# A decoder block in fp32r: SwiGLU in four parts instead of three, with the down products among the next part's blocks, seven of eleven hidden blocks in seven products, three lent PSUM banks and edges of order

## The chip, the cores and the metric

The kernel runs on one core of one Trainium2 chip. The metric is the device time of one execution in microseconds (us). Three executions of the kernel before took 1533.85, 1528.16 and 1534.53 us, median 1533.85. The engines are named as the profile names them: PE is TensorE, which multiplies; DVE is VectorE; ACT is ScalarE; POOL is GpSimd; SP is SyncE, which issues the weight loads.

## The reference

One decoder block on 256 tokens of width 2048, in float32. Cut to what matters:

```python
h = x + mixer(rmsnorm(x))          # w_in: 2048 x 16400, w_out: 2048 x 2048
h = h + swiglu(rmsnorm(h))         # w_gate_up: 2048 x 11264, w_down: 5632 x 2048
return rmsnorm(h)

def mixer(h):
    q, k, v, g_out, gk_low, gate_b, gate_c, xc, merge_a, merge_b = split(h @ w_in)
    # log decays from gk_low; chunked causal gated linear attention over 4 heads
    o = gla_chunked(q, k, v, log_sigmoid(gk_low @ w_gk_up + b_gk_up) / 16)
    y_a = rmsnorm(o) * silu(g_out)
    y_b = gate_b * causal_conv3(gate_c * xc)
    return (sigmoid(merge_a) * y_a + sigmoid(merge_b) * y_b) @ w_out

def swiglu(h):
    gate, up = split(h @ w_gate_up)          # 5632 columns each
    return (silu(gate) * up) @ w_down
```

## The kernel before, in words

**Three products for one.** A float32 product is made of three fp32r products. Each operand is split in a high part, rounded to fp32r, and a low part, the rest. `mm3` (L324 to L328) multiplies token-high by weight-low (L326), token-low by weight-high (L327) and high by high (L328) into one PSUM bank. In a row of the profile the weights stand first: `dn<-lo,acth` is L326.

**Pieces.** The weights are streamed in pieces of 128 partitions x 1024 floats (512 KB): two chunks of 128 rows by 512 columns. For each piece SP issues the load into `raw`, ACT makes the high part (L217) and DVE subtracts it to make the low part (L222). `take` (L314) keeps five pieces loaded ahead of the one in use (`LOOK = 5`); `raw` and `lo` have five buffers each, `hi` six. A plain piece costs PE 12 matmuls of 512 columns: two halves of the tokens (t = 0, 1), two chunks, three products.

**Eights and sevens.** A block is 512 columns of the gate and the same 512 of the up matrix, 16 plain pieces, 192 matmuls. The function `eights` (L354) does one matrix of it, in two PSUM banks, one for each half of the tokens. The function `sevens` (L374) does gate and up of one block together in seven products instead of eight (Strassen's scheme in Winograd's form, on token halves and row chunks): 28 pieces of 6 matmuls, 168 matmuls, in five banks `b0` to `b4`. For 16 of the 28 pieces the weights must first be added on DVE (`sum_of`, L238 and L244), and afterwards five results are combined on DVE (L398 to L411). `mixed` (L106) puts plain pieces between those of a seven: one behind each piece that needed a sum, the rest among the last eight.

**The order.** A list written out by hand (`stream_list`, L157) sets the order of all pieces: the attention's k, q and v columns; the gates (24 groups of 512 columns, four pairs of them in sevens); w_out; then SwiGLU. SwiGLU is done in three parts of 4, 4 and 3 blocks (`PARTS`, L69). In each part first the hidden blocks, some in sevens with others as eights between them (`HIDDEN`, L82: blocks 0, 2, 4, 6 and 9 in sevens), and then all down products of that part (`down_list`, L141), whose sums DVE adds to `h` (L1044). Small work is tied to the count of pieces used, the tick: `later` and `at` run a function at a tick, `one_at_a_time` runs the transposes of finished hidden blocks two ticks apart. A scheduler then arranges the instructions of each engine into its fixed order, and may move an instruction ahead of others that were written earlier.

**PSUM.** There are eight banks. `b0` to `b4` serve sevens. During gates and hidden blocks the eights always use `b5` and `ax1`, and the transposes `ax0` (L354 and L543). The down products take `b0` to `b5` in turn.

**Attention.** At ticks 20 to 25 tables of decays are made: POOL prepares `exk` and `exq` (L686 to L690), ACT takes the exponentials of four tables (L678, L691, L692, L705). `decayed` (L726) multiplies q and k by them, `scores` (L730) makes scores on PE and copies them out with a mask (L742 on DVE, L743 and L745 on ACT, L747 on DVE), and `attend` (L754) multiplies them by v into `o_ps`. `x_blocks` (L711, ticks 42, 47, 52, 57) makes the sums and differences of x that the gates' sevens need, on DVE (L715, L438, L440) and ACT (L439).

**The end.** The last 512 columns of the last part are two groups of 256. The second of them is done for t = 0 first and then for t = 1; `finish(t)` (L942) normalises and stores each half.

## Time and profile before

| what | value |
|---|---|
| median of three executions | 1533.85 us (1528.16 to 1534.53) |
| the profiled execution | 1535.26 us |
| its span, first to last instruction | 1533.6 us |
| PE busy | 1510.4 us, 98% of the span |
| DVE busy | 1173.5 us, 77% |
| ACT busy | 832.1 us, 54% |
| HBM read over the span | 338.45 MB, 222 GB/s with the writes |
| SwiGLU on PE, first to last matmul | 822 to 1526 us |

How to read it: busy time is the union of an engine's instructions. A matmul of 512 columns is recorded as 0.389 us long, but the next one starts before it ends, so the price of a matmul on PE is the time from start to start, which is had by dividing a stretch in which PE never waits by the matmuls in it. A view by waits names, for each engine and line, who released it and for how long it had been idle. A view by windows gives busy time, counts, the granted TensorE clock and the DMA traffic of stretches of the span.

### The profile page before, as it was taken

The page shows a single profiled execution, that of the slowest core. Times are in us where ns is not written, and L with a number is a line of the kernel's source. Part 1 is how long each engine was busy: PE and PEld are TensorE (multiplying, and loading weights), DVE is VectorE, ACT ScalarE, POOL GpSimd, SP SyncE. Part 2 cuts the span into 40 slices and gives each one's busy share as a digit, 9 for nine tenths or more (in the row PEclk, how much of TensorE's full clock was granted, in tenths as well). Part 3 has the DMA queues.
Part 4 walks back from the last instruction along what each step waited for, and adds up shares of the span by engine and source line. Part 5 has one row for each costly group of instructions (what it writes and reads, how often), then busy time and mean ns, then how long its engine had stood idle before and what let it go on. Part 6 is the DMA issues. An engine that isn't in the chain of part 4 may idle for free.

```text
span 1533.6 us, 19370 instructions
## 1 busy us (share of the span) xinstructions
PE 1510.4 (98%) x7153; PEld 1262.0 (82%) x7153; DVE 1173.5 (77%) x1173; ACT 832.1 (54%) x936; POOL 36.6 (2%) x61
## 2 busy tenths in 40 slices
PE   9989999999999999999999999999999999999998
PEld 8979988888787788878788888888888888888887
DVE  5787557979879879965668899855889975678764
ACT  6755445555654555654556555633555653455543
POOL 0020000000000000000000000000000000000000
PEclk9999999999999999999999999999999999999999
DMA  9645557878776888786765767866677886566872
GB/s 321 222 150 158 172 158 248 276 228 259 260 246 212 286 261 257 242 263 206 224 178 178 263 221 250 312 200 178 219 248 224 273 272 192 178 229 197 249 222 92
DMA packets 96399, 346.00 MB, mean 226 GB/s; under 512 B 11092, under 2 KB 11220, under 8 KB 96176
## 3 DMA queue, kind: packets, MB, share of 16 engines
q1 hardware_dynamic: 92928, 333.77, 68.0%
q0 software_dynamic: 2944, 9.41, 2.5%
q10 hardware_dynamic: 432, 1.57, 0.3%
q8 instruction: 56, 0.92, 0.2%
q14 instruction: 39, 0.32, 0.1%
HBM read 338.45 MB, written 2.10 MB: 222 GB/s over the span
## 4 chain that ended last, share of the span: by engine, by line
PE 92%; DVE 3%; issue 1%; ACT 1%; DMA 1%; POOL 1%; SPq 0%; DVEq 0%; ACTq 0%
PE fg L326 7%; PE fg L328 7%; PE fg L327 7%; PE dn L326 5%; PE dn L327 5%; PE dn L328 5%; PE gc L326 3%; PE fu L326 3%; PE fu L328 3%; PE fu L327 3%; PE gc L328 3%; PE gc L327 3%; PE gb L326 2%; PE wo L326 2%; PE mb L326 2%; PE gb L327 2%
## 5 line engine op out<-in xcount | busy, mean ns | idle before, releaser
L222 DVE TENSOR_TENSOR lo<-raw,hi 128x1024 fp32r<-128x1024 f32 (+1 forms) x517 | 628.1, 1219 | 231.3 <-PE dn L326 74.8
L217 ACT CAST hi<-raw 128x1024 fp32r<-128x1024 f32 (+1 forms) x517 | 539.9, 1050 | 409.1 <-PE dn L328 114.1
L217 ACT CAST hi<-x 128x1024 fp32r<-128x1024 f32 x108 | 113.7, 1053 | 185.6 <-DVE x L244 130.0
L222 DVE TENSOR_TENSOR lo<-x,hi 128x1024 fp32r<-128x1024 f32 x108 | 132.1, 1223 | 31.8 <-ACT hi L217 18.7
L326 PE MATMUL dn<-lo,acth 128*128 128x512 f32 (+1 forms) x376 | 141.7, 377 | 0.0
L328 PE MATMUL dn<-hi,acth 128*128 128x512 f32 (+1 forms) x376 | 141.3, 376 | 0.0
L327 PE MATMUL dn<-hi,actl 128*128 128x512 f32 (+1 forms) x376 | 141.2, 376 | 0.0
L326 PE MATMUL fg<-lo,hh 128*128 128x512 f32 x312 | 121.6, 390 | 0.0
L328 PE MATMUL fg<-hi,hh 128*128 128x512 f32 x312 | 121.5, 389 | 0.0
L327 PE MATMUL fg<-hi,hl 128*128 128x512 f32 x312 | 121.4, 389 | 0.0
L244 DVE TENSOR_TENSOR x<-x,raw 128x1024 f32<-128x1024 f32 x72 | 87.9, 1220 | 7.2 <-DMA raw<-in_w_in_dram 3.5
L328 PEld LDWEIGHTS dn<-hi,acth 128*128 128x128 f32 x376 | 70.8, 188 | 13.0
L326 PEld LDWEIGHTS dn<-lo,acth 128*128 128x128 f32 x376 | 70.8, 188 | 12.7
L327 PEld LDWEIGHTS dn<-hi,actl 128*128 128x128 f32 x376 | 70.8, 188 | 12.6
L328 PE MATMUL fu<-hi,hh 128*128 128x512 f32 x192 | 74.7, 389 | 0.0
L326 PE MATMUL fu<-lo,hh 128*128 128x512 f32 x192 | 74.7, 389 | 0.0
L327 PE MATMUL fu<-hi,hl 128*128 128x512 f32 x192 | 74.7, 389 | 0.0
L326 PEld LDWEIGHTS fg<-lo,hh 128*128 128x128 f32 x312 | 58.6, 188 | 12.5 <-DVE h L1044 0.3
L328 PEld LDWEIGHTS fg<-hi,hh 128*128 128x128 f32 x312 | 58.6, 188 | 12.4
L327 PEld LDWEIGHTS fg<-hi,hl 128*128 128x128 f32 x312 | 58.6, 188 | 12.1
L326 PE MATMUL fg<-lo,sh 128*128 128x512 f32 x160 | 63.8, 399 | 0.0
L328 PE MATMUL fg<-hi,sh 128*128 128x512 f32 x160 | 62.5, 391 | 0.0
(245 smaller groups left out, 3067.8 us busy)
## 6 DMA issues: line engine op xcount, KB each, us to landing
raw<-in_w_in_dram SPq DMA_DIRECT2D x255, 512.0 KB, 4.6
raw<-in_w_gu_dram SPq DMA_DIRECT2D x176, 512.0 KB, 4.4
raw<-in_w_dn_dram SPq DMA_DIRECT2D x88, 512.0 KB, 4.3
raw<-in_w_out_dram SPq DMA_DIRECT2D x32, 512.0 KB, 4.2
x<-in_w_gu_dram SPq DMA_DIRECT2D x20, 512.0 KB, 5.4
y<-in_w_gu_dram SPq DMA_DIRECT2D x20, 512.0 KB, 3.9
y<-in_w_in_dram SPq DMA_DIRECT2D x16, 512.0 KB, 4.2
x<-in_w_in_dram SPq DMA_DIRECT2D x16, 512.0 KB, 4.9
```

The costliest lines, as they stand in the source:

```text
L217: nc.scalar.copy(hi[:, ks, :], raw[:, ks, :])
L222: nc.vector.tensor_tensor(out=lo[:, ks, :], in0=raw[:, ks, :], in1=hi[:, ks, :].bitcast(F32), op=ALU.subtract)
L244: nc.vector.tensor_tensor(out=x, in0=x, in1=other, op=ALU.add)
L326: nc.tensor.matmul(ps, lhsT=sh, rhs=ml, start=first, stop=False, skip_group_check=onto)
L327: nc.tensor.matmul(ps, lhsT=sl, rhs=mh, start=False, stop=False, skip_group_check=onto)
L328: nc.tensor.matmul(ps, lhsT=sh, rhs=mh, start=False, stop=last, skip_group_check=onto)
```

## The change

Four things are changed.

**SwiGLU.** Parts of 3, 3, 3 and 2 blocks. Blocks 0, 3, 4, 6, 7, 9 and 10 are done in sevens. The others (1, 2, 5 and 8) and the down products of the first three parts form one list of plain pieces (`PLAIN`), of which each seven takes a number (`SEVENS`: 19, 19, 19, 19, 21, 17, 16). So a part's down products stand between the pieces of the next part's sevens. The last six down pieces of the third part follow the last seven; the fourth part's down products come at the end as before. A transpose of block f waits until the down products of block f - 4, whose buffer it takes, are through (`free_at`).

**Three lent banks.** `b5`, `ax0` and `ax1` form a queue. An eights group, and now a down group, takes the two at its front and gives them back at its end; a transpose takes the front one and puts it at the back. The rest of the program's turn goes over `b0` to `b4`.

**Edges of order.** `pin` keeps the written order of the first instruction of `x_blocks`, of the convolution's and of the merge's instructions on DVE, and `issue_after` puts the exponentials of `exk` and `exq` behind those of `ek` and `eq` on ACT.

**Ticks.** `x_blocks` runs at ticks 50, 54, 58 and 62.

```diff
-PARTS = ((0, 4), (4, 8), (8, 11))
+PARTS = ((0, 3), (3, 6), (6, 9), (9, 11))
...
-HIDDEN = (
-    ((("fg0", "fu0"), ("fg1", "fu1")), (("fg2", "fu2"), ("fg3", "fu3"))),
-    ((("fg4", "fu4"), ("fg5", "fu5")), (("fg6", "fu6"), ("fg7", "fu7"))),
-    ((("fg9", "fu9"), ("fg8", "fu8", "fg10", "fu10")),),
-)
+SEVENS = ((0, 19), (3, 19), (4, 19), (6, 19), (7, 21), (9, 17), (10, 16))
+PLAIN = (1, 2, (0, (1, 0, 2)), 5, (1, (3, 4, 5)), 8, (2, (6, 7, 8)))
...
+def hidden_list():
+
+    plain = []
+    for what in PLAIN:
+        if isinstance(what, tuple):
+            part, fs = what
+            plain += [e for n in range(len(DOWN[part])) for f in fs for e in down_of(part, n, f)]
+        else:
+            plain += [(f"{name}{what}", k) for name in ("fg", "fu") for k in range(0, KC, 2)]
+    out = []
+    for f, n in SEVENS:
+        out += mixed((f"fg{f}", f"fu{f}"), plain[:n])
+        plain = plain[n:]
+    return out + plain
...
-            tag = f"b{turn['b'] % 6}"
+            tag = f"b{turn['b'] % turn['of']}"
...
+    lent = ["b5", "ax0", "ax1"]
...
-    def eights(key, a, done, tags=("b5", "ax1")):
-
-        ps = [bank([P, 512], f"{key}_{t}", tag) for t, tag in enumerate(tags)]
+    def eights(key, a, done, tags=None):
+
+        mine = tags or [lent.pop(0) for _ in range(NT)]
+        ps = [bank([P, 512], f"{key}_{t}", tag) for t, tag in enumerate(mine)]
...
         done(ps)
+        if tags is None:
+            lent.extend(mine)
...
     def transpose_block(src, t, hi, lo):
 
-        ps = bank([P, 4, P], "trb", "ax0")
+        lent.append(lent.pop(0))
+        ps = bank([P, 4, P], "trb", lent[-1])
...
-        nc.scalar.activation(exk, exk, AF.Exp, scale=inv)
-        nc.scalar.activation(exq, exq, AF.Exp, scale=inv)
+        with tc.issue_after(first_exp[-1]):
+            nc.scalar.activation(exk, exk, AF.Exp, scale=inv)
+            nc.scalar.activation(exq, exq, AF.Exp, scale=inv)
...
-        nc.vector.tensor_tensor(out=raw, in0=xh[:, cs, :].bitcast(F32), in1=xl[:, cs, :].bitcast(F32), op=ALU.add)
+        pin(nc.vector.tensor_tensor(out=raw, in0=xh[:, cs, :].bitcast(F32), in1=xl[:, cs, :].bitcast(F32), op=ALU.add))
...
-        at(42 + 5 * q, lambda q=q: x_blocks(q))
+        at(X_AT[q], lambda q=q: x_blocks(q))
...
     def put(delay, f, src, t):
-        one_at_a_time(delay, lambda: transpose_block(src, t, *act_of(f)))
+        one_at_a_time(max(delay, free_at.get(f - 4, 0) - count["tick"]), lambda: transpose_block(src, t, *act_of(f)))
...
+    def down(key):
+
+        part, n = (int(s) for s in key[2:].split("_"))
+        cs = slice(DOWN[part][n][0], sum(DOWN[part][n]))
+        mine = [lent.pop(0) for _ in range(NT)]
+        ps = [bank([P, cs.stop - cs.start], f"{key}_{t}", tag) for t, tag in enumerate(mine)]
+        number = sum(e[0] == key for e in order)
+        for i in range(number):
+            piece, k0 = yield
+            for t in range(NT):
+                tok_piece(ps[t], t, piece, k0, i == 0, i == number - 1, hidden_act(part))
+        for t in range(NT):
+            nc.vector.tensor_tensor(out=h[:, t, cs], in0=ps[t], in1=h[:, t, cs], op=ALU.add)
+        lent.extend(mine)
...
+X_AT = (50, 54, 58, 62)
```

What this does to the order of the engines is seen at three places. A row is a line of the source, an operation, what it writes and reads, and a count where a row repeats; in the changed kernel the same line stands further down (L222 is L230, L244 is L252, L742 is L758).

The first place is ACT's queue at the decay tables. Before:

```order
L217 CAST hi<-raw 128x1024 x4
L691 ACT_TABLE_LOAD
L691 ACTIVATE exk<-exk 128x1024
L692 ACTIVATE exq<-exq 128x1024
L678 ACTIVATE ek<-eq 128x2048
L217 CAST hi<-raw 128x1024
L705 ACTIVATE eq<-eq 128x2048
L217 CAST hi<-raw 128x1024 x5
```

Now:

```order
L225 CAST hi<-raw 128x1024 x4
L693 ACT_TABLE_LOAD
L693 ACTIVATE ek<-eq 128x2048
L225 CAST hi<-raw 128x1024
L721 ACTIVATE eq<-eq 128x2048
L225 CAST hi<-raw 128x1024
L707 ACTIVATE exk<-exk 128x1024
L708 ACTIVATE exq<-exq 128x1024
L225 CAST hi<-raw 128x1024 x5
```

The two exponentials whose input POOL makes stood ahead of the two whose input DVE makes; they now stand behind them.

The second place is DVE's queue between the products of head 1 with the decay tables and the scores that are copied out of PSUM (`scr` is a score tile, `scl` its low part, `xraw` and `sl` belong to `x_blocks`). Before:

```order
L726 TENSOR_TENSOR exk<-exk,kr 128x256
L715 TENSOR_TENSOR xraw<-xh,xl 128x1024
L222 TENSOR_TENSOR lo<-raw,hi 128x1024
L438 TENSOR_TENSOR xraw<-xraw 128x256 x3
L222 TENSOR_TENSOR lo<-raw,hi 128x1024
L438 TENSOR_TENSOR xraw<-xraw 128x256
L222 TENSOR_TENSOR lo<-raw,hi 128x1024
L440 TENSOR_TENSOR sl<-xraw,sh 128x1024
L742 COPY_PREDICATED scr<-mask,sc_ps 128x256
L715 TENSOR_TENSOR xraw<-xh,xl 128x1024
L747 TENSOR_TENSOR scl<-scr,sch 128x384
```

Now:

```order
L742 TENSOR_TENSOR exk<-exk,kr 128x256
L230 TENSOR_TENSOR lo<-raw,hi 128x1024 x3
L758 COPY_PREDICATED scr<-mask,sc_ps 128x256
L763 TENSOR_TENSOR scl<-scr,sch 128x384
L230 TENSOR_TENSOR lo<-raw,hi 128x1024
L758 COPY_PREDICATED scr<-mask,sc_ps 128x256
L763 TENSOR_TENSOR scl<-scr,sch 128x384
```

The instructions of `x_blocks` have left this place for one some 20 pieces later.

The third place is DVE's queue where the second part's first down group ends (`h<-dn` is the addition of its sums to `h`, once for each half of the tokens). Before, in the stretch of down products alone:

```order
L222 TENSOR_TENSOR lo<-raw,hi 128x1024 x10
L1044 TENSOR_TENSOR h<-dn_0_0_10249,h 128x512
L222 TENSOR_TENSOR lo<-raw,hi 128x1024
L1044 TENSOR_TENSOR h<-dn_0_1_10250,h 128x512
L222 TENSOR_TENSOR lo<-raw,hi 128x1024
L1044 TENSOR_TENSOR h<-dn_1_0_10287,h 128x512
```

Now, among the pieces of block 7's seven:

```order
L252 TENSOR_TENSOR x<-x,raw 128x1024
L561 TENSOR_TENSOR actl<-trb,acth 128x4x128
L246 TENSOR_TENSOR raw<-y,x 128x1024
L230 TENSOR_TENSOR lo<-x,hi 128x1024
L230 TENSOR_TENSOR lo<-raw,hi 128x1024
L1021 TENSOR_TENSOR h<-dn_0_0_9676,h 128x512
L1021 TENSOR_TENSOR h<-dn_0_1_9677,h 128x512
L230 TENSOR_TENSOR lo<-y,hi 128x1024
L230 TENSOR_TENSOR lo<-raw,hi 128x1024
```

The additions now stand between the low parts and the sums of weights of a seven, and the banks that they free are two of the three lent ones, where before they were two of six.

More of the change, by code (lines that the diff above doesn't have):

```diff
@@ L103, in seven_list, with mixed @@
     return [(pair, e) for e in out + list(twos)]
-def mixed(step, early=False):
-    pair, keys = step
-    eights = [(key, k) for key in keys for k in range(0, KC, 2)]
+def mixed(pair, eights, early=False):
     if pair is None:
@@ L160, in stream_list @@
     out = [e for e in pieces if e[0][0] in "kqv"] + gates_list() + [e for e in pieces if e[0][:2] == "wo"]
-    for part in range(len(PARTS)):
-        out += hidden_list(part) + down_list(part)
-    return out
+    return out + hidden_list() + down_list()
 @with_exitstack
@@ L527, in transpose_gain @@
         for m in range(2):
-            ps = aux([P, 2, T], "tr")
+            lent.append(lent.pop(0))
+            ps = bank([P, 2, T], "tr", lent[-1])
             for j in range(2):
@@ L541, in transpose_block @@
     def transpose_block(src, t, hi, lo):
-        ps = bank([P, 4, P], "trb", "ax0")
+        lent.append(lent.pop(0))
+        ps = bank([P, 4, P], "trb", lent[-1])
         for j in range(4):
@@ L914, in block_kernel @@
     h = None
+    turn["of"] = 5
     for n in range(4):
@@ L967, in block_kernel @@
     act = {}
+    order = hidden_list()
+    base = count["tick"]
+    free_at = {f: base + 2 + max(i for i, e in enumerate(order) if e in down_of(p, len(DOWN[p]) - 1, f))
+               for p, fs in enumerate(PARTS[:-1]) for f in range(*fs)}
     def act_of(f):
@@ L1005, in hidden @@
         return eights(key, whole(hh, hl), gate_done)
-    finb = None
-    for part, (f0, f1) in enumerate(PARTS):
-        count["gap"] = 2
-        for _ in run(hidden_list(part), hidden):
-            pass
-        count["gap"] = 1
-        if part == len(PARTS) - 1:
-            finb = sT.tile([P, D], F32, tag="sh", name="finb")
-            nc.scalar.dma_start(finb, finw.to_broadcast([P, D]))
-        down = down_list(part)
-        of = {n: [e for e in down if e[0] == f"dn{part}_{n}"] for n in range(len(DOWN[part]))}
-        pd, kept = {}, {}
-        def hidden_act(t, k):
-            hi, lo = act_of(f0 + k // 4)
-            ts = slice(t * P, (t + 1) * P)
-            return hi[:, k % 4, ts], lo[:, k % 4, ts]
-        for e in down:
-            key, k0 = e
-            n = int(key.split("_")[1])
-            c0, w = DOWN[part][n]
-            cs = slice(c0, c0 + w)
-            last = part == len(PARTS) - 1 and n == nd - 1
-            if e == of[n][0]:
-                pd[n] = [bank([P, w], f"{key}_{t}") for t in range(NT)]
-            piece = take(key, k0)
-            if last:
-                kept[e] = piece
-                if e != of[n][-1]:
-                    continue
-            for t in range(NT):
-                for g in (of[n] if last else [e]):
-                    tok_piece(pd[n][t], t, kept[g] if last else piece, g[1], g == of[n][0], g == of[n][-1], hidden_act)
-                if e != of[n][-1]:
-                    continue
-                nc.vector.tensor_tensor(out=h[:, t, cs], in0=pd[n][t], in1=h[:, t, cs], op=ALU.add)
-                if part == len(PARTS) - 1:
-                    square_sum(h[:, t, cs], ssf[:, t, n:n + 1])
-                    if not last:
-                        nc.vector.tensor_tensor(out=h[:, t, cs], in0=h[:, t, cs], in1=finb[:, cs], op=ALU.mult)
-                    else:
-                        finish(t)
-            if not last:
-                used()
@@ new lines, in block_kernel @@
+    count["gap"] = 2
+    for _ in run(order, hidden):
+        pass
+    count["gap"] = 1
+    finb = sT.tile([P, D], F32, tag="sh", name="finb")
+    nc.scalar.dma_start(finb, finw.to_broadcast([P, D]))
+    part = len(PARTS) - 1
+    order = down_list()
+    of = {n: [e for e in order if e[0] == f"dn{part}_{n}"] for n in range(nd)}
+    acts = hidden_act(part)
+    pd, kept = {}, {}
+    for e in order:
+        key, k0 = e
+        n = int(key.split("_")[1])
+        c0, w = DOWN[part][n]
+        cs = slice(c0, c0 + w)
+        last = n == nd - 1
+        if e == of[n][0]:
+            pd[n] = [bank([P, w], f"{key}_{t}") for t in range(NT)]
+        piece = take(key, k0)
+        if last:
+            kept[e] = piece
+            if e != of[n][-1]:
+                continue
+        for t in range(NT):
+            for g in (of[n] if last else [e]):
+                tok_piece(pd[n][t], t, kept[g] if last else piece, g[1], g == of[n][0], g == of[n][-1], acts)
+            if e != of[n][-1]:
+                continue
+            nc.vector.tensor_tensor(out=h[:, t, cs], in0=pd[n][t], in1=h[:, t, cs], op=ALU.add)
+            square_sum(h[:, t, cs], ssf[:, t, n:n + 1])
+            if not last:
+                nc.vector.tensor_tensor(out=h[:, t, cs], in0=h[:, t, cs], in1=finb[:, cs], op=ALU.mult)
+            else:
+                finish(t)
+        if not last:
+            used()
```

48 lines of the change are left out of this document (27 added, 21 removed).

## The prediction

> **What bounds the kernel now.** I read the page first, then busy time by windows, then the waits of PE.
>
> ```profile
> PE 1510.4 (98%) x7153; PEld 1262.0 (82%) x7153; DVE 1173.5 (77%) x1173; ACT 832.1 (54%) x936; POOL 36.6 (2%) x61
> ```
>
> PE is busy 98% of 1533.6 us. Two windows split off SwiGLU; five of its stages follow (hidden blocks and down products of the first part, the same of the second, then the third's hidden blocks).
>
> ```profile
> 0.00:822.00 822.00, 806.42 (x3937) 676.95 (x3938) 630.18 (x652) 458.67 (x530) 36.65 (x61) 1.00 0.72 228
> 822.00:1526.00 704.00, 703.95 (x3218) 585.09 (x3216) 541.36 (x518) 371.94 (x402) 0.00 (x0) 1.00 0.70 222
> ...
> 822.00:989.50 167.50, 167.50 (x757) 138.46 (x756) 155.20 (x149) 104.84 (x117) 0.00 (x0) 1.00 0.77 252
> 989.50:1076.50 87.00, 87.00 (x387) 72.03 (x386) 49.04 (x46) 35.35 (x35) 0.00 (x0) 1.00 0.63 192
> 1076.50:1244.00 167.50, 167.50 (x753) 138.41 (x752) 153.02 (x143) 99.08 (x105) 0.00 (x0) 1.00 0.78 253
> 1244.00:1331.00 87.00, 87.00 (x387) 72.04 (x386) 48.11 (x45) 34.77 (x34) 0.00 (x0) 1.00 0.66 197
> 1331.00:1457.00 126.00, 126.00 (x564) 104.30 (x563) 96.01 (x87) 68.75 (x70) 0.00 (x0) 1.00 0.70 222
> ```
>
> Columns after the length: busy us and count of PE, weight loads, DVE, ACT, POOL; then clock, DMA share, GB/s. In SwiGLU PE never stops, though DVE is busy 155.2 of 167.5 us in one stage and 49.0 of 87 in the next. So there only fewer matmuls help. Ahead of it PE idles 15.6 us; the waits tell for whom.
>
> ```profile
> PE gb L326 <- DVE ya L844: 3.0, 3, 1.5
> PE o_ps L326 <- ACT sch L745: 2.9, 1, 2.9
> PE o_ps L326 <- ACT scr L743: 1.8, 1, 1.8
> PE g L326 <- DVE sb L844: 1.4, 1, 1.4
> PE tr L532 <- DVE h L925: 1.4, 1, 1.4
> ...
> PE ma L326 <- ACT ya L853: 1.0, 1, 1.0
> PE gc L326 <- ACT ya L853: 0.8, 1, 0.8
> PE trb L545 <- DVE sb L833: 0.5, 1, 0.5
> ```
>
> Attention's `o_ps` waits 4.7 us; the gate groups (`gb`, `g`, `ma`) 5.4 us, for the release of banks `b5` and `ax1`.
>
> **Fewer matmuls.** Two more blocks go from 192 to 168 matmuls: 48 fewer. One costs
>
> ```profile
> 1000.00:1100.00 100.00, 100.00 (x442) 82.59 (x441) 63.20 (x58) 41.91 (x40) 0.00 (x0) 1.00 0.62 190
> ```
>
> 100/442 = 0.226 us, so -10.9 us. The last part has two blocks, not three: 48 fewer matmuls of 256 columns, 24 more of 512. The 36 narrow ones of the last group run under the rows below, from 1521.67 (t = 0 is complete) to 1525.98, 0.12 us each: -5.8 + 5.4 = -0.4 us.
>
> **The tail gives some back.**
>
> ```profile
> 1521.67 0.42 DVE L1044 TENSOR_TENSOR h<-dn,h 128x256 f32<-128x256 f32 x1 [2.56 <-PE dn L328]
> 1522.72 1.28 ACT L949 ACT_TABLE_LOAD   x1
> 1525.34 0.61 DVE L958 TENSOR_SCALAR h<-h,r 128x768 f32<-128x768 f32 x1
> 1525.98 0.42 DVE L1044 TENSOR_TENSOR h<-dn,h 128x256 f32<-128x256 f32 x1
> ```
>
> DVE's chain of `finish(0)` ends at 1525.95, just as PE ends t = 1; now t = 1 has 24 matmuls, ends 1.4 us sooner, and still stands behind that chain. So 12 x 0.12 = 1.4 us of the saving is lost: +1.4.
>
> **Attention.** DVE's and ACT's rows at the stall:
>
> ```profile
> 85.65 1.06 ACT L691 ACTIVATE exk<-exk 128x1024 f32<-128x1024 f32 x1 [7.20 <-POOL exk L687]
> ...
> 102.72 0.42 DVE L438 TENSOR_TENSOR xraw<-xraw 128x256 f32<-128x256 f32 x1
> 103.17 1.05 ACT L439 CAST sh<-xraw 128x1024 fp32r<-128x1024 f32 x1 [5.59 <-DVE xraw L438]
> 104.25 1.23 DVE L440 TENSOR_TENSOR sl<-xraw,sh 128x1024 fp32r<-128x1024 f32 x1
> 105.40 0.43 DVE L742 COPY_PREDICATED scr<-mask,sc_ps 128x256 f32<-128x256 int8 x1
> 105.86 0.27 ACT L743 COPY scr<-sc_ps 128x128 f32<-128x128 f32 x1 [0.70 <-DVE scr L742]
> 106.16 0.51 ACT L745 CAST sch<-scr 128x384 fp32r<-128x384 f32 x1
> 106.72 0.49 PE L326 MATMUL o_ps<-vl,sch 128*128 128x512 f32 x1 [2.89 <-ACT sch L745]
> ```
>
> Two things made the score copy late: ACT stood 7.2 us at `exk` for POOL with `ek` and `eq` behind it, and the x_blocks rows L715, L438 and L440 stood ahead of L742. Both leave, as the first two places of the order show. Without an x_blocks chain (L715 and L440 at 1.22, four L438 at 0.42: 4.1 us) the score copy falls at 105.40 - 4.1 = 101.3 at the latest, and `sch` is ready 1.3 us later, at 102.6; PE needs it at 106.72 - 2.89 = 103.8. The second score copy stands behind one more low part, so I leave 1.0 us: 4.7 becomes 1.0, -3.7 us (bounds 0 and -4.7). The work of x_blocks moves under the matmuls of heads 2 and 3, where DVE has room:
>
> ```profile
> 100.00:200.00 100.00, 95.08 (x603) 86.04 (x603) 69.07 (x92) 50.33 (x67) 0.94 (x3) 0.97 0.58 171
> 200.00:300.00 100.00, 98.76 (x435) 81.10 (x434) 76.69 (x70) 54.82 (x62) 1.88 (x3) 1.00 0.70 226
> ```
>
> So its move costs 0; if that room is gone, see the first rival.
>
> After the stall the clock was halved.
>
> ```profile
> 110.00:115.70 5.70, 5.70 (x14) 4.44 (x15) 5.48 (x8) 4.97 (x10) 0.31 (x1) 0.50 0.50 172
> ```
>
> 14 matmuls where 5.7/0.226 = 25 fit: 11 x 0.226 = 2.5 us, which go with the stall: -2.5 (or 0).
>
> [...]
>
> **Gate banks.** With three banks the next group's t = 0 has a free bank, and needs the old group's first bank only 6 matmuls (1.4 us) later; waits of at most 1.5 us nearly vanish. 5.4 becomes 0.8: -4.6 (bounds 0 and -5.4). The pinned rows of merge and convolution keep the written order; PE waited for them 0.5 us in all (`trb`, quoted): 0. The waits of `gc`, `tr` and `trb` stay.
>
> **Handovers in SwiGLU.** Twelve down groups change hands there on lent banks. The add stands behind low parts four pieces ahead, as the third place shows. A bank whose t = 0 sums are complete is next needed as the new group's t = 1 bank. Between lie 18 matmuls, 4.1 us: the old group's t = 1 half, one piece of a seven, the new group's t = 0 half. If the add slips further, PE stands with the sevens' pieces queued behind it. Bounds: 0, as in `fg` and `fu` of before, which shared two fixed banks and show in no row of waits; and 1.5 each, as in `gb`. I take 0, the nearer row.
>
> **DVE and DMA.** Each new seven adds 12 low parts and 16 sums. Is DVE still hidden? Its step:
>
> ```profile
> 906.50 1.22 DVE L244 TENSOR_TENSOR x<-x,raw 128x1024 f32<-128x1024 f32 x1
> 907.64 0.68 DVE L411 TENSOR_TENSOR u<-fg,v 128x512 f32<-128x512 f32 x1
> ```
>
> 1.14 us from start to start. The small work of a plain block is two rows of each of these:
>
> ```profile
> L548 DVE TENSOR_TENSOR actl<-trb,acth 128x512 fp32r<-128x512 f32 x22 | 15.1, 688 | 5.2 <-ACT acth L547 5.0
> L965 DVE SCALAR_TENSOR_TENSOR sg<-fu,r,sg 128x512 f32<-128x512 f32 x12 | 8.9, 743 | 0.0
> ```
>
> A seven with one plain block took, by the hidden stage of the second part, 153.0/2 = 76.5 us of DVE against 83.75 of PE. Without the block (16 x 1.14 + 2 x 0.69 + 2 x 0.74 = 21.1; on PE 16 x 2.72 = 43.5) it is 55.4 against 40.2. A down piece took 49.04/32 = 1.53 against 87/32 = 2.72. The new stretch has four sevens with a block, three without, and 66 down pieces: DVE 306 + 166 + 101 = 573 us, PE 335 + 121 + 180 = 636. That is 90%, no more than the 91 to 93% that two stages of 167.5 us bore with PE at 100%, far longer than five pieces of lead (some 10 us) could carry: 0. ACT gets 24 more casts and stays near its 60% of those stages: 0. Sixteen more loads of 512 KB stand in SP's queue; the stretch asks for no more per us than those stages (253 GB/s at a DMA share of 0.78): 0. If DVE's cover is gone, see the second rival.
>
> [...]
>
> **Sum.** -10.9 - 0.4 + 1.4 - 3.7 - 2.5 - 4.6 = -20.7 us. The profiled execution took 1535.26, its span 1533.6; that becomes 1514.6. The median of the runs shown is 1533.85, 1.4 less: **1513**.
>
> **Rivals.** *The early stall only moves* (12%): x_blocks, now at ticks 50 to 62, meet the scores of head 2 or 3, and the stall with its half clock stays. For it: they are still whole chains across DVE and ACT (ACT waited 5.59 us at L439). Against: DVE is idle there for a quarter of the time. 1513 + 3.7 + 2.5 = 1519.
>
> *DVE becomes the bound* (12%): 90% is a mean, and pieces are uneven; in the gates
>
> ```profile
> 400.00:500.00 100.00, 96.99 (x428) 78.89 (x427) 89.73 (x84) 55.18 (x58) 4.97 (x9) 1.00 0.76 241
> ```
>
> DVE at 90% went with PE at 97%. At that loss, 3% of 636 = 19 us, the time is 1532, no change. Against: those idle spots have bank waits as their rows.
>
> *Slower by bank release* (7%): DVE, 90% busy and without the rest that pure down stages gave it (49.0 of 87 us), reaches each add late, and PE stands at each handover of a lent pair, 12 down and 8 gate or up groups. It decides against the change from 1 us each (20.7/20). At `gb`'s 1.5: 30 - 20.7 = +9, 1543. Against: the 4.1 us of room.
>
> **Chances.** Forecast 66%, the three rivals 12, 12 and 7, 3% for others. About 0.5% (7.7 us) can be told from no change. Faster by more: 66 + 12 and the milder half of DVE's case and others, 82%; within 0.5%: 11%; slower: 7%. The likeliest case alone reaches from 1507 to 1518; the range takes in the moved stall, half of DVE's case, and below it the runs' own spread (1528.16 - 24 = 1504): 1504 to 1527.
>
> **What would show it.** Right: no half clock near 110; `o_ps` under 1 us; `gb`, `g` and `ma` gone from PE's waits; PE 100% in the stretch of sevens, with DVE near 90%; 72 fewer matmuls; still 12 us from the add of t = 0 (1521.67) to the end. Wrong: PE waiting for DVE's low parts there (DVE's bound), PE's `dn` waiting for the add (banks), or the half clock elsewhere.

## The result, and the profile after

The changed kernel took 1507.41 us, the median of four executions (1506.61 to 1507.71), against 1533.3 us for the kernel before in four (1528.16 to 1534.53): a ratio of 0.9837, with a 95% interval of 0.9814 to 0.986. The profiled execution took 1506.61 us, its span is 1504.9.

The busy times of the page, then three windows (all ahead of SwiGLU, SwiGLU's matmuls, the stretch in which sevens stand), with columns as in the prediction:

```profile
PE 1491.5 (99%) x7081; PEld 1249.3 (83%) x7081; DVE 1247.7 (83%) x1247; ACT 859.1 (57%) x962; POOL 38.5 (3%) x61
```

```profile
0.00:803.70 803.70, 799.20 (x3938) 674.43 (x3939) 633.44 (x652) 458.97 (x530) 38.47 (x61) 1.00 0.73 233
803.70:1496.00 692.30, 692.30 (x3145) 574.91 (x3143) 610.95 (x588) 397.92 (x427) 0.00 (x0) 1.00 0.75 238
...
803.70:1434.20 630.50, 630.50 (x2824) 521.92 (x2823) 573.97 (x541) 370.71 (x387) 0.00 (x0) 1.00 0.77 246
```

The page counts 7081 matmuls where it had 7153: 72 fewer, as worked out. PE never stops in SwiGLU, although DVE is busy 573.97 of 630.50 us, 91%, in the stretch of sevens. Ahead of it PE stood 15.6 us; now it stands 803.70 - 799.20 = 4.5. The waits of PE, all that the view lists:

```profile
PE warm_ps L487 <- DVE spare L483: 1.3, 1, 1.3
PE g L334 <- DVE lo L230: 1.0, 1, 1.0
PE k L334 <- ACT hi L225: 0.5, 1, 0.5
PE gc L334 <- DVE lo L230: 0.5, 1, 0.5
PE k L335 <- DVE lo L230: 0.4, 2, 0.2
PE tr L544 <- DVE h L942: 0.4, 1, 0.4
PE k L334 <- DVE xl L506: 0.2, 1, 0.2
```

`o_ps`, `gb`, `ma` and `trb` are gone. What is left of `g` waits for a low part, not for a bank. The stall of attention, by windows over the same times as before, and the first masked score copy on DVE (L758 now, at 105.40 before):

```profile
100.00:115.70 15.70, 15.70 (x96) 14.04 (x94) 8.83 (x13) 12.06 (x23) 0.31 (x1) 1.00 0.49 153
100.00:200.00 100.00, 100.00 (x635) 91.08 (x634) 68.66 (x90) 50.63 (x67) 0.62 (x2) 1.00 0.57 172
```

```profile
96.28 0.43 DVE L758 COPY_PREDICATED scr<-mask,sc_ps 128x256 f32<-128x256 int8 x1
```

PE is busy throughout and the clock is whole; it was at 0.50 from 110 to 115.7. The tail, DVE's rows:

```profile
1493.19 0.42 DVE L1084 TENSOR_TENSOR h<-dn,h 128x256 f32<-128x256 f32 x1 [1.12 <-PE dn L336]
...
1496.86 0.61 DVE L975 TENSOR_SCALAR h<-h,r 128x768 f32<-128x768 f32 x1
1497.38 0.42 DVE L1084 TENSOR_TENSOR h<-dn,h 128x256 f32<-128x256 f32 x1
```

From the add of t = 0 to the end it is 1504.9 - 1493.19 = 11.7 us (11.9 before). PE ends at 1496.0, and the add of t = 1 stands behind the chain of `finish(0)` until 1497.38.

The next table divides the spans by stage, always from the start of one matmul to the start of another (attention from the first `v` to the last, gates from there to the first `wo`, w_out to the first `fg`, SwiGLU from there to the last `dn`, the tail to the end). It is worked out from the rows of the traces; one profiled execution each, in us. The runs in it are told of below.

| kernel | start | attention | gates | w_out | SwiGLU | tail | median time |
|---|---|---|---|---|---|---|---|
| before | 35.2 | 177.9 | 516.3 | 92.7 | 703.5 | 7.9 | 1533.3 |
| the change | 34.3 | 169.2 | 508.6 | 91.5 | 692.1 | 9.1 | 1507.41 |
| a1_issue | 35.1 | 172.3 | 515.7 | 91.7 | 703.5 | 7.9 | 1529.35 |
| a2_xblocks | 34.6 | 169.2 | 514.6 | 91.7 | 703.6 | 7.9 | 1524.39 |
| a4_banks | 34.9 | 176.9 | 510.6 | 91.7 | 704.4 | 7.9 | 1527.55 |
| a5_pins | 34.7 | 177.5 | 513.4 | 92.0 | 703.5 | 7.9 | 1529.94 |
| a7_front | 34.6 | 169.2 | 509.4 | 92.2 | 704.5 | 7.9 | 1519.58 |
| b3_twobanks | 34.7 | 169.2 | 510.9 | 92.8 | 692.4 | 9.1 | 1511.61 |

By the spans the change gains 28.7 us: 8.7 in attention, 7.7 in the gates, 11.4 in SwiGLU, 1.2 in w_out, 0.9 at the start, less 1.2 in the tail. By the medians it is 25.9: the profiled execution of before (1535.26) lies 2.0 us above its median, that of the change 0.8 below.

How far single executions differ can be read from eight kernels that have the same code ahead of SwiGLU: the change, a7, d1, d2, b1, c1, c2 and e3. Worked out in the same way, attention takes 169.2 us in each, but the start takes 34.3 to 35.4 us, the gates 507.1 to 509.5 and w_out 91.5 to 92.9. The three kernels that leave the gates as they were (before, a1 and a2) take 514.6 to 516.3 us there. So the gains of attention, gates and SwiGLU are clear of this spread; those of w_out and the start are not.

### The profile page after: what moved, and what is told of

It is laid out like the page before. It is cut to its first block, busy times and chain, and to the rows that moved or that the text cites. A ratio compares the mean times of both kernels' runs of the same rounds, so it can differ in the third digit from the quotient of the medians.

```text
span 1504.9 us, 19344 instructions
## 1 busy us (share of the span) xinstructions
PE 1491.5 (99%) x7081; PEld 1249.3 (83%) x7081; DVE 1247.7 (83%) x1247; ACT 859.1 (57%) x962; POOL 38.5 (3%) x61
## 4 chain that ended last, share of the span: by engine, by line
PE 96%; DVE 1%; DMA 1%; issue 1%; ACT 1%; SPq 0%; DVEq 0%; ACTq 0%
PE fg L336 8%; PE fg L334 8%; PE fg L335 8%; PE dn L334 5%; PE dn L336 5%; PE dn L335 5%; PE gc L334 3%; PE gc L335 3%; PE gc L336 3%; PE v L335 2%; PE wo L334 2%; PE v L334 2%; PE gb L334 2%; PE gb L335 2%; PE v L336 2%; PE gb L336 2%
## 5 line engine op out<-in xcount | busy, mean ns | idle before, releaser
L230 DVE TENSOR_TENSOR lo<-raw,hi 128x1024 fp32r<-128x1024 f32 (+1 forms) x509 | 618.6, 1220 | 148.1 <-ACT hi L225 31.8
L225 ACT CAST hi<-raw 128x1024 fp32r<-128x1024 f32 (+1 forms) x509 | 531.6, 1050 | 326.3 <-PE dn L336 43.8
L225 ACT CAST hi<-x 128x1024 fp32r<-128x1024 f32 x132 | 139.0, 1053 | 208.6 <-DVE x L252 140.2
L230 DVE TENSOR_TENSOR lo<-x,hi 128x1024 fp32r<-128x1024 f32 x132 | 161.3, 1222 | 27.0 <-ACT hi L225 19.5
L252 DVE TENSOR_TENSOR x<-x,raw 128x1024 f32<-128x1024 f32 x88 | 107.3, 1219 | 9.1 <-DMA raw<-in_w_in_dram 7.5
L334 PE MATMUL fg<-lo,sh 128*128 128x512 f32 x224 | 88.0, 393 | 0.0
L336 PE MATMUL fg<-hi,sh 128*128 128x512 f32 x224 | 87.3, 390 | 0.0
L335 PE MATMUL fg<-hi,sl 128*128 128x512 f32 x224 | 87.2, 389 | 0.0
L334 PEld LDWEIGHTS fg<-lo,hh 128*128 128x128 f32 x296 | 55.6, 188 | 11.4
L230 DVE TENSOR_TENSOR lo<-y,hi 128x1024 fp32r<-128x1024 f32 x44 | 53.7, 1219 | 10.0 <-PE fu L334 3.6
L225 ACT CAST hi<-y 128x1024 fp32r<-128x1024 f32 x44 | 46.2, 1050 | 16.9 <-PE fg L336 5.4
```

Source lines behind the costliest of these rows:

```text
L225: nc.scalar.copy(hi[:, ks, :], raw[:, ks, :])
L230: nc.vector.tensor_tensor(out=lo[:, ks, :], in0=raw[:, ks, :], in1=hi[:, ks, :].bitcast(F32), op=ALU.subtract)
L252: nc.vector.tensor_tensor(out=x, in0=x, in1=other, op=ALU.add)
L334: nc.tensor.matmul(ps, lhsT=sh, rhs=ml, start=first, stop=False, skip_group_check=onto)
L335: nc.tensor.matmul(ps, lhsT=sl, rhs=mh, start=False, stop=False, skip_group_check=onto)
L336: nc.tensor.matmul(ps, lhsT=sh, rhs=mh, start=False, stop=last, skip_group_check=onto)
```

## The experiments

Two theories stood behind the prediction: the parts of the change act in separate stages and add up; and DVE, 91% busy, stays hidden in SwiGLU. Runs a1 to b3 test the first, the others the second.

**The two late things in attention, one at a time.** Each is added to the kernel before. a1_issue:

```diff
-        nc.scalar.activation(exk, exk, AF.Exp, scale=inv)
-        nc.scalar.activation(exq, exq, AF.Exp, scale=inv)
+        with tc.issue_after(first_exp[-1]):
+            nc.scalar.activation(exk, exk, AF.Exp, scale=inv)
+            nc.scalar.activation(exq, exq, AF.Exp, scale=inv)
```

> The kernel before with one edit: the exponentials of exk and exq are issued on ACT behind those of ek and eq. Theory 1 (two late things in series, either of which alone would have been hidden): DVE's decay products start 7 us earlier, the x_blocks rows still stand ahead of the score copy but run earlier, PE's wait at o_ps falls from 4.7 us to under 1 us and the half clock near 110 us goes; the span falls by 6 to 8 us. Theory 2 (the x_blocks chain alone makes the stall): the wait stays above 3 us, the half clock stays, the span falls by less than 2 us. SwiGLU keeps 704 us and the gates their waits in both.

a2_xblocks:

```diff
-        nc.vector.tensor_tensor(out=raw, in0=xh[:, cs, :].bitcast(F32), in1=xl[:, cs, :].bitcast(F32), op=ALU.add)
+        pin(nc.vector.tensor_tensor(out=raw, in0=xh[:, cs, :].bitcast(F32), in1=xl[:, cs, :].bitcast(F32), op=ALU.add))
-        at(42 + 5 * q, lambda q=q: x_blocks(q))
+        at(X_AT[q], lambda q=q: x_blocks(q))        # 50, 54, 58, 62
```

> The kernel before with one edit: x_blocks at ticks 50, 54, 58 and 62 with its first row held in written order; ACT still stands 7 us at exk. Theory 1 (either alone): the score copy comes by 101.3 us, o_ps waits at most 1 us, no half clock, span 6 to 8 us shorter. Theory 3 (ACT's wait at exk is the cause): o_ps still waits 3 us or more and the half clock stays.

Measured against 1531.98 us for the kernel before on the same chip: a1 1529.35, ratio 0.998 (0.9969 to 0.9991); a2 1524.39, 0.9959 (0.9945 to 0.9974). Of a1 the two waits of PE at `o_ps` and the window after the stall; of a2 the same window, and its first score copy with ACT's wait for `exk`:

```profile
PE o_ps L326 <- DVE vl L796: 1.3, 1, 1.3
...
PE o_ps L326 <- ACT scr L746: 1.2, 1, 1.2
```

```profile
108.00:116.00 8.00, 6.69 (x41) 5.73 (x40) 7.93 (x13) 7.90 (x14) 0.00 (x0) 1.00 0.44 132
```

```profile
108.00:116.00 8.00, 8.00 (x61) 7.63 (x60) 5.75 (x9) 6.38 (x13) 0.00 (x0) 1.00 0.46 133
```

```profile
81.51 1.06 ACT L692 ACTIVATE exk<-exk 128x1024 f32<-128x1024 f32 x1 [3.69 <-POOL exk L688]
...
98.22 0.43 DVE L743 COPY_PREDICATED scr<-mask,sc_ps 128x256 f32<-128x256 int8 x1
```

With x_blocks moved alone the whole stall is gone, and attention is as short as in the changed kernel (169.2 us). But ACT stands only 3.69 us for `exk` in this execution, not 7.20, and the edit isn't the reason: POOL's first subtraction for `exk`, ahead of any row of x_blocks, was short this time. Before, and in a2:

```profile
77.53 6.08 POOL L686 TENSOR_TENSOR exk<-bc 128x512 f32<-128x512 f32 x1 [26.90 <-DVE bc L670]
```

```profile
76.89 1.93 POOL L687 TENSOR_TENSOR exk<-bc 128x512 f32<-128x512 f32 x1 [26.89 <-DVE bc L671]
```

It takes 1.93 us in the traces of a2, b3 and d2 and 6.07 or 6.08 in all others, those of the change and of a7 among them, which move x_blocks, too. So a2's trace shows a later x_blocks and half of the `exk` wait gone together. An estimate: with the long subtraction the score copy would come up to 7.20 - 3.69 = 3.5 us later, at 101.7, and `sch` at 103.0; PE needed it at 103.8 before, and a2 started 0.6 us earlier. The stall would just be hidden, without room to spare. a2's four executions lie within 2.4 us of each other, but there is no trace of a2 with the long case.

The issue order alone brings the score copy from 105.40 to 100.75 and keeps the clock whole (1.00 from 108 to 116). At the place of the stall PE waits 1.2 us instead of 4.7; 1.3 us come anew ten us later, where the low part of v (`vl`) stands on DVE behind rows of x_blocks and others. So the expectation holds for a2; for a1, where either alone was to suffice, it fails by the 2.5 us that stay. x_blocks on DVE was the larger of the two. a1's median is only 2.6 us better while its stage is 5.6 us shorter; the profiled execution of before, from which the stage is counted, was 3.3 us longer than the median of these 25 (1531.98).

**Banks alone, pins alone.** a4_banks is the kernel before with the list of three lent banks for eights and transposes, and five banks in turn from w_out on (the edits of `eights`, `transpose_block` and `bank` in the change's diff). a5_pins wraps the rows of convolution and merge in `pin(...)`.

> The kernel before with three lent banks for eights and transposes, and nothing else. By the prediction's term the waits of gb, g and ma (5.4 us) fall to 0.8 and the gates, which took 516.3 us from v's last matmul to w_out's first, take 4.6 us less; attention's stall and SwiGLU (704 us) stay. Rival: the gates' 7.7 us that the changed kernel saved come from the edges of order, and banks alone give under 2 us.

> The kernel before with the convolution's and the merge's DVE instructions held in written order, and nothing else. By the prediction 0 us. Rival: DVE no longer stands at the convolution's shifted loads (7.8 us of idle at L827 before), its low parts come earlier, and the gates take 2 to 4 us less, which is what the prediction missed there.

a4 took 1527.55 us, 0.9967 (0.9953 to 0.9981); a5 1529.94, 0.999 (0.9978 to 1.0001). Of a4, PE's waits and two windows, the stall with what follows it and the part of it at half clock; of a5, the waits of the gates:

```profile
PE o_ps L327 <- ACT sch L751: 2.9, 1, 2.9
PE trb L551 <- DVE sb L839: 1.8, 1, 1.8
PE o_ps L327 <- ACT scr L749: 1.3, 1, 1.3
...
PE gc L327 <- ACT ya L859: 0.7, 1, 0.7
```

```profile
108.00:116.00 8.00, 6.71 (x24) 5.15 (x24) 7.74 (x14) 6.50 (x12) 0.31 (x1) 0.69 0.48 132
106.20:112.90 6.70, 5.16 (x11) 3.32 (x12) 6.51 (x11) 4.60 (x8) 0.62 (x2) 0.50 0.48 149
```

```profile
PE gb L327 <- DVE ya L845: 2.5, 3, 1.5
PE g L327 <- DVE sb L845: 1.6, 1, 1.6
```

With three banks `gb`, `g` and `ma` leave the list; the gates lose 5.7 us and the median 4.4, as priced. None of the eight kernels with the change's front has `gb` or `ma` on its list, or `g` for anything but a low part. The wait of `trb` for `sb`, which the merge writes, grows from 0.5 to 1.8; pinned as in the change it is absent in some traces and still 0.9 in d1 and 1.1 in a7. The pins alone take `ma` and `trb` off the list. Their gates are 2.9 us shorter than those of before but only 1.2 shorter than a2's, which touches no gate, and the whole time is not told from no change by its interval. So the pins are worth between nothing and 3 us, more likely something than nothing. In a4 the stall stays, and so does the half clock: 0.69 is the mean of a window that it fills in part.

**All but SwiGLU.** a7_front has every part of the change that lies ahead of SwiGLU, and SwiGLU as before.

> The kernel before with everything of the change that lies ahead of SwiGLU (issue order of exk and exq, the later ticks of x_blocks, the pins, the three lent banks), and SwiGLU's own order and parts as before. Theory 1 (the parts add up and SwiGLU's saving is separate): the two front stages lose 8.7 and 7.7 us and the output projection 1.2 as in the changed kernel's trace, SwiGLU stays at 703.5 us and the tail at 7.6: 17 us less than before, 0.989. Theory 2 (the parts overlap, or some of the front's gain comes from SwiGLU's new order or its banks): less than 12 us, or SwiGLU's own matmuls move by more than 1 us.

It took 1519.58 us against 1532.12, 0.9922 (0.9896 to 0.9948): 12.5 us. Its span is 15.9 us shorter than that of before, 1.1 less than expected (gates 509.4 instead of 508.6, SwiGLU 704.5 instead of 703.5). From it to the changed kernel SwiGLU falls by 12.4 us and the tail grows by 1.2. The measured 12.5 us lie between the figures of the two theories. By stages the parts add up; the sum of the expectation was taken from the long execution of before and is too large by its 3 us.

**Handovers on two banks.** b3_twobanks is the changed kernel with one fixed pair of banks for all eights and down groups. Besides the lines shown, the transposes `tr` go back to `ax0` and `ax1` in turn:

```diff
-    lent = ["b5", "ax0", "ax1"]
+    lent = ["b5", "ax1"]
...
-        lent.append(lent.pop(0))
-        ps = bank([P, 4, P], "trb", lent[-1])
+        ps = bank([P, 4, P], "trb", "ax0")
```

> The changed kernel with two lent banks (b5, ax1) in place of three, and the transposes back on ax0; SwiGLU in four parts with seven sevens stays. It puts all handovers, 8 of gate or up groups and 12 of down groups among the sevens, on one fixed pair. Theory 1 (a fixed pair's adds come within a handover's room in SwiGLU, as fg and fu did before): the gates lose again 4 to 5 us, SwiGLU loses under 2 us; 1512 to 1514 us. Theory 2 (with DVE 91% busy each handover on a fixed pair costs up to the 1.5 us that gb showed): dn shows in PE's waits, 12 to 20 times 1.5 us, SwiGLU loses 10 to 30 us; 1525 or more. That would show that the third bank is a condition of the new order.

It took 1511.61 us, 0.987 (0.9847 to 0.9892). SwiGLU by windows, and the waits of the gates and of w_out that returned:

```profile
807.70:1500.10 692.40, 692.40 (x3145) 574.62 (x3143) 610.88 (x587) 398.19 (x427) 0.00 (x0) 1.00 0.72 238
```

```profile
PE gb L334 <- DVE ya L858: 1.7, 2, 1.5
PE tr L543 <- DVE h L940: 1.6, 2, 1.4
...
PE g L334 <- DVE sb L858: 0.8, 1, 0.8
```

Even on a fixed pair the handovers cost PE nothing in SwiGLU: 692.4 us busy of 692.4. The rival of slowness by bank release falls, and the third bank is needed only ahead of SwiGLU. In the gates it is worth about 2 us beside the pins: b3's take 2.3 us more than the change's and 1.4 more than the longest of the eight kernels with its front. The theory expected 4 to 5 there, so pins and banks seem to remove partly the same waits.

**How much room DVE has.** d1 and d2 compute a low part twice, with the same result, for 28 and for 56 of the sevens' pieces. For d1 these are the pieces of product 11 (weights as they come); for d2, shown here, those of product 11 and of t2 (a sum made in place in x):

```diff
         low(raw, piece)
+        if isinstance(k0, tuple) and key[0][:2] == "fg" and k0[0] in ('11', 't2'):
+            low(raw, piece)
```

> The changed kernel with 28 more VectorE operations in the stretch of sevens: the low part of the first piece of each four (product 11) is computed twice with the same result; nothing else moves. 28 x 1.14 = 32 us of VectorE. Theory 1 (the sum alone counts, VectorE can be busy to the end): 573.8 + 32 = 606 of 630.3 us, no change, 0 to 3 us more than the changed kernel. Theory 2 (VectorE stands 1.2 us for ScalarE's cast behind most in-place sums, and so carries no more than 92 to 93% of the time, as in the runs with 56 more and with the eighth seven): 606/0.925 = 655, 25 us more, less what the waits overlap: 14 to 25 us more. At 56 more operations 49 us were added; if the edge is sharp, 28 fewer of 1.14 us give 49 - 32 = 17.

> The changed kernel with 56 more VectorE operations in the stretch of sevens: for two of the four kinds of sevens' pieces that are hit, the low part is computed twice, the second time with the same result; nothing else moves. It measures VectorE's room there. At 1.14 us a step they are 64 us; the changed kernel's trace leaves 630.3 - 573.8 = 56.5 us. Theory 1 (the room is usable to the end, only the sum counts): 64 - 56 = 8 us more, 0 to 12. [...] Theory 3 (91% is a mean over uneven stretches and VectorE is already bound locally): 25 to 64 us more.

d1 took 1510.14 us, 0.9861 (0.9841 to 0.9881); d2 1556.54, 1.0163 (1.014 to 1.0186). The stretch of sevens of d1 and of d2 by windows, and DVE's longest wait in d1 and in d2 from 860 to 1430 (15.3 us in 42 places in the changed kernel):

```profile
805.70:1438.00 632.30, 631.45 (x2824) 521.68 (x2823) 594.88 (x567) 358.29 (x385) 0.00 (x0) 1.00 0.73 243
```

```profile
804.70:1484.10 679.40, 648.24 (x2828) 516.70 (x2827) 626.01 (x595) 355.41 (x385) 0.00 (x0) 1.00 0.69 226
```

```profile
DVE lo L230 <- ACT hi L225: 22.6, 26, 1.2
```

```profile
DVE lo L230 <- ACT hi L225: 34.9, 35, 1.3
```

With 28 more operations DVE is busy 94% and the stretch is 1.8 us longer (the whole times of d1 and of the change are not told apart by their intervals); with 56 it is 48.9 us longer. DVE's 626.01 us of work would have fitted into 630.5, yet 53.4 us of idle time came on top. Where it lies d2's rows show:

```profile
1108.22 1.22 DVE L230 TENSOR_TENSOR lo<-x,hi 128x1024 fp32r<-128x1024 f32 x1
1109.35 1.22 DVE L246 TENSOR_TENSOR raw<-y,x 128x1024 f32<-128x1024 f32 x1
1110.49 1.22 DVE L252 TENSOR_TENSOR x<-x,raw 128x1024 f32<-128x1024 f32 x1
1112.87 1.22 DVE L230 TENSOR_TENSOR lo<-x,hi 128x1024 fp32r<-128x1024 f32 x1 [1.17 <-ACT hi L225]
```

An in-place sum of x stands directly ahead of its own low part, which needs ACT's cast of the sum: DVE stands 1.2 us. Such neighbours, counted in the stretch: 2 of 82 sums in the changed kernel (2.4 us idle), 18 in d1 (21.4), 32 in d2 (38.0). So neither the sum alone (8 us expected for d2) nor a fixed ceiling of 92 to 93% (14 to 25 us expected for d1) is right; d2's 49 us lie in the range of its third theory, but d1 excludes that DVE was bound already. The room took 28 operations for 1.8 us, and did not take 56. Number and place changed together, though: the 28 that d2 adds to those of d1 stand between a sum of x and the next one, and 28 of these alone were not run. So a sharp edge in the amount of work is not shown. The step of 1.13 to 1.14 us stays where DVE is the bound (1108.22, 1109.35, 1110.49), so d2's loss is not that of a longer step.

**An eighth seven.** b1_eight puts block 5 in seven products, too:

```diff
-SEVENS = ((0, 19), (3, 19), (4, 19), (6, 19), (7, 21), (9, 17), (10, 16))
-PLAIN = (1, 2, (0, (1, 0, 2)), 5, (1, (3, 4, 5)), 8, (2, (6, 7, 8)))
+SEVENS = ((0, 18), (3, 17), (4, 11), (5, 10), (6, 14), (7, 15), (9, 15), (10, 14))
+PLAIN = (1, 2, (0, (1, 0, 2)), (1, (3, 4, 5)), 8, (2, (6, 7, 8)))
```

> The changed kernel with an eighth block in seven products (block 5), its pieces among down products and plain blocks as the others'. 24 matmuls fewer: 24 x 0.226 = 5.4 us less PE; VectorE gets 55.4 - 21.1 = 34 us more, 608 of 625 us in the stretch, 97%. Two of the sevens (blocks 4 and 5) have only 10 or 11 plain pieces beside them, where by the prices of the prediction VectorE needs 103 to 105% of PE's time. Theory 1 (work is carried over a few pieces, the sum counts): 2 to 5 us less than the changed kernel. Theory 2 (VectorE bound where plain pieces are scarce): the gain is eaten, 0 to 10 us more than the changed kernel, with low parts as PE's waits among blocks 4 and 5.

It took 1535.76 us, 1.0031 (1.0018 to 1.0044): 28 us more than the changed kernel, with 24 matmuls fewer. Its stretch of sevens and PE's first wait:

```profile
804.80:1463.40 658.60, 638.62 (x2800) 515.49 (x2799) 601.90 (x573) 372.40 (x399) 0.00 (x0) 1.00 0.72 240
```

```profile
PE fg L334 <- DVE lo L230: 16.4, 25, 2.6
```

The loss is larger than either theory gave. PE is busy 139.98 of 140 us from 860 to 1000, 148.41 of 160 from 1000 to 1160 and 264.19 of 270 from there to 1430. So the loss begins near blocks 4 and 5, where plain pieces are scarce (by the prices of the prediction an estimated 980 to 1118 us), but goes on behind them; 21 of 94 sums are neighbours of their own low part (24.9 us idle).

**Relief by GpSimd.** c1_eightpool is b1_eight with the first of each four sums on POOL, which does nothing in SwiGLU. c2_ninepool has nine sevens and two of four sums on POOL; the line of its second sum is changed in the same way. The edit that both have:

```diff
-            nc.vector.tensor_tensor(out=raw, in0=y, in1=held["x"], op=ALU.add)
+            (nc.gpsimd if one[:2] == "fg" else nc.vector).tensor_tensor(out=raw, in0=y, in1=held["x"], op=ALU.add)
```

> Eight sevens as in the run that was slower, and of each four sums the first (t1, into a raw buffer) on GpSimd, which does nothing in SwiGLU. GpSimd's 128x512 subtraction took 1.5 us, so 3 us each by that price, 32 of them. VectorE: 608 - 32 x 1.14 = 571 of 625 us, 91% as in the changed kernel. Theory 1 (VectorE's load was all that stood against the eighth seven): its 24 matmuls come free, 1507 - 5.4 = 1502 us. Theory 2 (few plain pieces beside blocks 4 and 5 fail for another reason, weight transfers or the lead of five pieces): 1515 to 1535. Theory 3 (GpSimd's sum comes late or slows VectorE): VectorE's rows longer than 1.22 us, or its low parts waiting for POOL; between the two.

> Nine sevens (all blocks but 1 and 5), 11 or 12 plain pieces beside each, with two of the four sums (t1 and t2) on GpSimd: 72 of 3 us each, 216 us. PE: 2 x 24 x 0.226 = 10.9 us less than the changed kernel. VectorE: 573.8 + 2 x 34.3 - 72 x 1.14 = 560 of 619 us, 90%. Theory 1 (the sum of VectorE's work, up to some 92%, is the limit): 1507 - 10.9 = 1496.5 us. Theory 2 (x is summed in place, so GpSimd's 3 us stand in a chain of sum, cast and low part in each four, or ACT and the transfers give out): low parts wait for POOL, 1500 to 1530 us.

c1 took 1536.19 us, 1.0032 (1.0018 to 1.0047), c2 1621.19, 1.0588 (1.0569 to 1.0606). Rows of c1, one sum on POOL and the low part on DVE beside it; then the group of low parts of x in c1:

```profile
1047.96 2.38 POOL L246 TENSOR_TENSOR raw<-y,x 128x1024 f32<-128x1024 f32 x1 [18.97 <-DVE lo L230]
1048.35 3.07 DVE L230 TENSOR_TENSOR lo<-raw,hi 128x1024 fp32r<-128x1024 f32 x1
```

```profile
L230 DVE TENSOR_TENSOR lo<-x,hi 128x1024 fp32r<-128x1024 f32 x82 | 123.0, 1500 | 27.8 <-ACT hi L225 24.0 <-PE dn L336 1.2 <-PE fu L334 0.9
```

This DVE operation, which meets a sum on POOL, lasts 3.07 us instead of 1.22. c1's trace has 31 of the 32 sums on POOL, 2.4 to 3.7 us long. Of the DVE operations of this size 57 overlap one of them and take 1.97 us on average, the other 847 take 1.22: 57 x 0.75, about 43 us more, where 32 x 1.14 = 36.5 were taken off. So the third theory's mechanism holds, DVE's rows are longer; its time, between 1502 and 1535, does not, for c1 is no faster than b1_eight (1535.76). With 20 of 94 sums still neighbours of their own low part (23.8 us idle), c1 doesn't show what a real relief of DVE would give. In the two rows shown, what the DVE row has too much, 3.07 - 1.22 = 1.85 us, is near what was left of POOL's row when it began (1047.96 + 2.38 - 1048.35 = 1.99); no run shows what makes a DVE row longer beside one of POOL.

c2 lies far outside both of its theories. The mechanism of the second is seen, the chain of a sum on POOL, the cast and the low part; ACT's and DVE's waits of c2 from 860 to 1430:

```profile
ACT hi L225 <- POOL x L252: 108.1, 26, 6.1
```

```profile
DVE lo L230 <- ACT hi L225: 81.3, 40, 3.6
```

PE's clock in that window is 0.96 on the mean; if the rest was at 1.00, that is an estimated 40 to 50 of the 570 us at 0.50, the one lower value that the clock takes in the traces of before and of the change. What each of the two costs was not separated.

**The written order on DVE.** e3_eightpin is b1_eight with SwiGLU's sums and low parts pinned in the order in which they are written:

```diff
+    def block(key):
+        return (key[0] if isinstance(key, tuple) else key)[:2] in ("fg", "fu", "dn")
...
+        ins = nc.vector.tensor_tensor(out=lo[:, ks, :], in0=raw[:, ks, :], in1=hi[:, ks, :].bitcast(F32), op=ALU.subtract)
+        if block(key):
+            pin(ins)
...
+        ins = nc.vector.tensor_tensor(out=x, in0=x, in1=other, op=ALU.add)
+        if block(pair):
+            pin(ins)
```

The first sum of each four, into `raw`, is pinned in the same way.

> Eight sevens as in the run that was slower, all sums on VectorE, and one thing more: in SwiGLU the sums and the low parts stand pinned in the order in which they are written. In the traces so far the place of slowness is a pair of neighbours on VectorE, an in-place sum of x with its own low part directly behind it, which stands 1.2 us for ScalarE's cast: 2 of 82 sums in the changed kernel, 18 with 28 more operations (21 us idle), 32 with 56 more (38 us), 21 of 94 with the eighth seven (25 us). In the written order another row stands between nearly all of them. Theory 1 (those neighbours are what made the eighth seven lose 28 us, with 5 us for the scarce plain pieces of blocks 4 and 5 on top): the idle time goes, 1507 - 5.4 + 5.4 = 1507, up to 1516 us. Theory 2 (scarce plain pieces or late weights are the cause, and the neighbours only show that VectorE is behind): 1528 to 1536 us, and VectorE waits for ScalarE or transfers elsewhere.

It took 1564.15 us against 1532.04, 1.0223 (1.0197 to 1.0249), 28 us more than b1_eight. DVE's waits from 860 to 1430, and a place:

```profile
DVE x L259 <- DMA raw<-in_w_gu_dram: 29.2, 16, 3.4
DVE sg L991 <- ACT sg L988: 13.0, 6, 3.7
DVE lo L233 <- ACT hi L228: 5.2, 9, 1.2
```

```profile
913.04 1.23 DVE L233 TENSOR_TENSOR lo<-raw,hi 128x1024 fp32r<-128x1024 f32 x1
916.05 1.22 DVE L259 TENSOR_TENSOR x<-x,raw 128x1024 f32<-128x1024 f32 x1 [1.78 <-DMA raw<-in_w_gu_dram]
```

The neighbours went (3 of 95 sums) and with them most of the low parts' waits for ACT (5.2 us; 31.6 in b1_eight), but in the fixed order DVE stands at sums whose weights have not come, at a DMA share of 0.67. So the neighbours are where the idle time lies when the scheduler sets the order, and taking them away in this manner only turns it into other waits. Part of the 28 us may be the clock: in four places of this stretch, 20.5 us in all, it is at 0.50 (3.4 us in b1_eight), which by the price of before, 14 matmuls where 25 fit, costs an estimated 20.5 x 11/25 = 9 us. Both theories fail in their numbers. What holds DVE below full use with eight sevens is therefore not settled: the round trip over ACT, the five buffers of weights and the scarce plain pieces were not separated.

## Why the prediction was right, point by point

The forecast was 1513 us; the time, 1507.41, lies in the range. Term by term, the stages of the table above beside the sum:

| term | forecast, us | trace, us |
|---|---|---|
| fewer matmuls and the last part | -11.3 | -11.4 |
| tail | +1.4 | +1.2 |
| `o_ps` and half clock | -6.2 | -8.7 |
| gates | -4.6 | -7.7 |
| w_out | 0 | -1.2 |
| start | 0 | -0.9 |
| handovers, DVE, DMA in SwiGLU | 0 | 0 |
| sum | -20.7 | -28.7 |

- **Fewer matmuls, and the tail**: right in mechanism and size. 72 matmuls are gone, and the chain of `finish(0)` still sets the end.
- **Attention**: the mechanism was right, the size too small by 2.5 us. The step that failed is "so I leave 1.0 us": the second score copy was to stand behind one more low part, and nothing stays. The score copy, forecast for "101.3 at the latest", came at 96.28, early enough to cover the low part. Another part of the 2.5 is the clock, priced from 110 us on: before, it was at 0.50 from 108.9. The rest was not separated. The prediction lets both late things leave; a2 shows no stall with x_blocks moved and half of the `exk` wait gone. Of the first rival (the stall only moves) nothing is seen in the change: 100 of 100 us busy from 100 to 200. a1, which leaves x_blocks where they were, shows a wait that moved.
- **The clock**: the half clock went with the stall, as the term said. What sets it off is not shown. Before, the clock is at 0.50 from 108.9 to 115.7, from within the second wait of `o_ps` (1.8 us, to 109.98), 2.2 us behind the end of the first (2.9 us, to 106.72). In a4 it is at 0.50 from 106.2 on; the wait of 2.9 us ended at 106.45 and the next, of 1.3 us, began only at 108.4, so only the first came before it. In a1 waits of 1.2 and 1.3 us, ten us apart, left the clock at 1.00. That it would stay whole beside the 1.0 us which the prediction left at `o_ps` was the author's estimate; a1's 1.2 us agrees with it. This made no difference to the time, since no wait of `o_ps` is left in the change. Whether the kernel before had the half clock in every execution is open: of its 25 executions on a1's chip the 7 with a mean granted clock of 0.998 or 0.999 took 1529.9 us on average, the 18 below that 1532.8.
- **Gates**: the banks were right (-4.6 forecast; 4.4 by a4's median, 5.7 by its trace), the stage too small by 3.1 us. The step that is in doubt is "The pinned rows of merge and convolution keep the written order", priced at 0: a5 shows `ma` and `trb` gone and gates 1.2 to 2.9 us shorter than those of the three kernels that leave them alone, which is near the spread. "The waits of `gc`, `tr` and `trb` stay" did not hold in the change's trace: `gc` for `ya` (0.8) and `trb` are gone, `tr` fell from 1.4 to 0.4. But these differ between kernels with the same front: `gc` waits 0.4 us for `ya` in a7, `tr` 0.4 to 1.6 us, `trb` nothing to 1.1.
- **w_out and the start**: 1.2 and 0.9 us that the prediction did not have; both lie within the spread of kernels with the same code there, and are luck of the two executions.
- **Handovers**: priced at 0 and 0 in the trace; b3 shows it even on a fixed pair. The third rival's waits at handovers do not occur.
- **DVE's cover**: 573 of 636 us were forecast, 573.97 of 630.50 measured, and PE at 100%. The term 0 was right. Its reason, a share of busy time below that of two earlier stages, was too simple: d2's 626 us of work did not fit in 630. The second rival was the nearest danger: d1, at 94%, lost 1.8 us, while d2 and one more seven are beyond the edge.
- **The reference execution**: the sum started from 1535.26 and 1.4 us were taken off for the distance to the median. 1535.26 - 28.7 = 1506.6 is the profiled execution of the change, and its median lies 0.8 above that. So the distance from 1513.2 (1513 before rounding) to 1507.41, 5.8 us, is 8.0 of terms that were too small or of luck, less 1.4 + 0.8 = 2.2 of this.
- **The chances**: "66 + 12 and the milder half of DVE's case and others" is 78 + 7.5 = 85.5, not 82%.
